# Queries projected by feature instead of by token in a fused gMLP and sliding-window attention trunk

## The chip, the core and the metric

The kernel runs on one core of a Trainium2 chip. A core has a matrix engine (TensorE, PE in the profile), a vector engine (VectorE, DVE), a scalar engine (ScalarE, ACT), GpSimd (POOL), and SyncE (SP), which here only issues transfers. Each engine works through its own queue in order, and semaphores tie the queues together. The metric is the device time of one execution in microseconds (us); the time of a kernel is the median of its runs.

## The reference

The input `x` has 2048 tokens of 1024 features in float32. Layer A is a gated MLP with a spatial mix over chunks of 128 tokens. Layer B is attention over a window of 128 tokens, with 16 query heads of 64 features, 2 key/value heads, rotary positions and one sink per head. What the change touches is the making of the queries in layer B:

```
z = rms_norm(h, b_norm_g) @ w_in          # (2048, 1024) @ (1024, 2048)
q, g = split(z, 2)
q = rotary((q + b_q) as 16 heads of 64, pos)
scores = q . k * 64**-0.5                 # each block of 128 queries against 256 keys
```

Rotary turns each head's features in two halves of 32: the first half becomes `x1*cos - x2*sin`, the second `x2*cos + x1*sin`.

## The kernel before

Activations lie with features on the partitions and tokens along the row, in float32. To keep accuracy with the faster matrix format, each operand is split in a high and a low part, and a product is three matmuls: high by high, high by low, low by high (`mm3`, lines 122 to 124).

Layer A takes the first part of the execution, up to about 1437 us. It also multiplies the weights of layer B by the norm's gain, splits them, and writes them back to memory (`pre_jobs` and `prescale`, lines 491 to 516; the multiply is line 504 on POOL). Layer B then runs four blocks of 512 tokens (loop at line 1140). In each block the list `PIECES` (line 53) gives the order of the projections: two pieces for keys and values (`k`), eight for queries (`q`, two for each of four quads of heads) and eight for the gate (`g`).

A clock `now` counts half pieces: `half()` (line 145) advances it by one and runs what is due. The scores of quad `q` and token tile `t` start at the half that `ATT` (line 54) gives, 11, 12, 14, 15 for the first quad, then 18, 20, 20, 22, then 23, 26, 28, 28, then 29, 31, 33, 35. `S_T` and `T_PV` halves later follow the transposes of the probabilities (line 1002) and the product with the values (line 1024). This is the order in which the program is written; the Tile scheduler decides, when the program is built, the fixed order in which each engine gets its instructions.

A `k` or `q` piece is token by feature: in `natural` (line 875) the activations of 128 tokens are the stationary operand and 256 columns of weights move, 24 matmuls for a token tile and 48 for a piece. A `q` piece holds four heads of two token tiles. DVE adds the bias (line 928) and rotates along the row (`rope`, lines 868 to 872); ACT and DVE split the result (lines 935 and 936). Three halves later (`Q_T`) TensorE transposes it, eight transposes a piece (line 943), and ACT copies it out (line 945), so that the features come to lie on the partitions, as the scores need them (lines 971 and 972).

A `g` piece is feature by token: `proj` (line 298) holds 128 by 128 weights stationary and moves 512 tokens, 24 matmuls for a piece, and ACT copies the bank out (line 951).

Weights come through `weights()`: it keeps three tiles ahead (`LOOKAHEAD`) in four buffers, and POOL issues the transfer (line 190). A `q` piece before takes two weight tiles for both of a quad's pieces. At the end of a block, `outproj_b` (line 1043) multiplies the gated attention by the output weights, which are split on ACT and DVE (lines 118 and 119). DVE also prepares the next block's normed activations there (`hn_steps`, line 323).

All temporary tiles of 128 by 512 come from one pool of 39 slots (`GEN_B`).

Of the kernel before, what the change touches and what calls it, by code (L numbers as in the profile page):

```python
# [12 lines left out]
F32 = mybir.dt.float32  # L13
# [5 lines left out]
P = 128  # L19
S = 2048  # L20
D = 1024
# [33 lines left out]
S_T = 4  # L55
T_PV = 3
K_T = 5
Q_T = 3
HN0 = 35


@with_exitstack
def trunk(ctx: ExitStack, tc: tile.TileContext, xT, wv, wug, wao, wkv, wqg, wbo, wsT, bs, gains, lngb,
          bq, bkv, sinks, rot, masks, out):
    nc = tc.nc
    V, A, G, PE = nc.vector, nc.scalar, nc.gpsimd, nc.tensor

# [265 lines left out]
    with ExitStack() as actx:  # L333
# [155 lines left out]


        pre_jobs = [(wkv[i], wkvD[i], kv_g[:, 4 * i:4 * i + 4], 4) for i in range(2)]
        pre_jobs += [(wqg[i], wqgD[i], b_g[:, 4 * (i % 2):4 * (i % 2) + 4], 4) for i in range(8)]
        pre_jobs += [(wqg[i], wqgD[i], b_g, 8) for i in range(8, 16)]

        def prescale(i):
            src, dst, g, nk = pre_jobs[i // 2]
# [350 lines left out]
    wraw[0] = ctx.enter_context(tc.tile_pool(name="raw", bufs=W_RAW_BUFS))  # L847
    msk = bc.tile([P, 3, P], F32, name="msk")
    nc.sync.dma_start(msk, masks)
    bq_sb = bc.tile([P, D], F32, name="bq_sb")  # L850
    nc.sync.dma_start(bq_sb, bq.partition_broadcast(P))
    bkv_sb = bc.tile([P, 256], F32, name="bkv_sb")
    nc.sync.dma_start(bkv_sb, bkv.partition_broadcast(P))
    sink_sb = bc.tile([P, 16], F32, name="sink_sb")
# [63 lines left out]

        after(K_T, turn)

    def q_piece(b, q, tp, w2, hh, hl, qT, tab):
        if not w2:
            w2.extend([weights(), weights()])
        ps = bank()
        for t2 in range(2):
            natural(ps, t2, 2 * tp + t2, w2, hh, hl)
        qs = slot()
        V.tensor_tensor(qs.rearrange("p (t n) -> p t n", t=2), ps.rearrange("p (t n) -> p t n", t=2),
                        bq_sb[:, None, q * 256:(q + 1) * 256].broadcast_to([P, 2, 256]), ALU.add)
        qr = rope(qs.rearrange("p (t h d) -> p t h d", t=2, h=4), 4, 2 * tp, 2, tab)  # L930
        qr = qr.rearrange("p (t h d) -> p t h d", t=2, h=4)
        sts = []
        for t2 in range(2):
            st = slot(F32R).rearrange("p (h s d) -> p h s d", h=4, s=2)
            A.copy(st[:, :, 0, :], qr[:, t2])
            V.tensor_tensor(st[:, :, 1, :], qr[:, t2], st[:, :, 0, :].bitcast(F32), ALU.subtract)
            sts.append(st)

        def turn():
            for t2 in range(2):  # L940
                pst = bank().bitcast(F32R)
                for h in range(4):
                    PE.transpose(pst[:, h * P:(h + 1) * P], sts[t2][:, h].rearrange("p s d -> p (s d)"), ident_r)  # L943
                t = slot(F32R)
                A.copy(t, pst.bitcast(F32))
                qT[4 * q + 2 * tp + t2] = t

        after(Q_T, turn)

    def g_piece(i, sg, hh, hl):  # L950
        A.copy(sg[:, i, :], proj(hh, hl))
# [1 line left out]
    def scores(b, q, t, qT):  # L953


        c = b * TT + t
        cur, prv = c % RING, (c - 1) % RING
        ic = int(cur != 0)
        band = slice(0, RING, RING - 1) if cur == 0 else slice(prv, cur + 1)
        kv = q // 2  # L960
        mx = sm.tile([P, 4], F32, name="mx")
        den = sm.tile([P, 4], F32, name="den")
        pn = slot()
        pss = []
        for par in range(2):
            ps = bank()
            for i in range(2):
                o = ps[:, i * 256:(i + 1) * 256]
                h = 2 * i + par
                lq = qT[4 * q + t][:, h * P:(h + 1) * P]  # L970
                PE.matmul(o, lq, kst[:, kv, 0, band, :], start=True, stop=False)  # L971
                PE.matmul(o, lq, kst[:, kv, 1, band, :], start=False, stop=True)  # L972
            s4 = ps.rearrange("p (i a k) -> p i a k", i=2, a=2)
            own, sel = s4[:, :, ic, :], s4[:, :, 1 - ic, :]
            if c == 0:
                V.copy_predicated(sel, msk[:, 1, None, :].broadcast_to([P, 2, P]).bitcast(I32),
                                  msk[:, 2, None, :].broadcast_to([P, 2, P]))
            V.copy_predicated(sel, msk[:, 0, None, :].broadcast_to([P, 2, P]).bitcast(I32), own)
            V.tensor_reduce(mx[:, 2 * par:2 * par + 2], sel, mybir.AxisListType.X, ALU.max)
            pss.append(sel)  # L980
        sk = sink_sb[:, 4 * q:4 * q + 4]
        m = sm.tile([P, 4], F32, name="m")
        V.scalar_tensor_tensor(m, mx, SC, sk, ALU.mult, ALU.max)
        nm = sm.tile([P, 4], F32, name="nm")
        V.tensor_scalar(nm, m, -1.0, None, ALU.mult)
        es = sm.tile([P, 4], F32, name="es")
        V.tensor_tensor(es, sk, m, ALU.subtract)
        for i in range(4):
            A.activation(pn[:, i * P:(i + 1) * P], pss[i // 2][:, i % 2, :], AF.Exp, bias=nm[:, i:i + 1], scale=SC,
                         accum_out=den[:, i:i + 1])  # L990
# [149 lines left out]
    for b in range(NB):  # L1140
        tab = slot().rearrange("p (a t d) -> p a t d", a=2, t=TT)
        nc.sync.dma_start(tab, rot[b])
        hh, hl = hn0
        qT, yh, yl = {}, {}, {}
        os_, sgs = {}, {}
        kvw, qw = [], {q: [] for q in range(NQ)}
        h0 = now[0]

        halves_done = [0] * NQ
# [30 lines left out]
        for p in PIECES:  # L1180
            kind, i, j = p[0], int(p[1]), int(p[2])
            if kind == "k":
                kv_piece(b, j, kvw, hh, hl, tab)
            elif kind == "q":
                q_piece(b, i, j, qw[i], hh, hl, qT, tab)
            else:
                if j == 0:
                    sgs[i] = qp.tile([P, 2, TB], F32, name="sg")
                g_piece(j, sgs[i], hh, hl)
                if j == 1:  # L1190
                    finish_quad(i)
# [5 lines left out]
def _layout(i):  # L1197
# [13 lines left out]
    wo = w_out.reshape(2, 2, 4, P, 2, 4, P)  # L1211
    a["wao"] = c(wo.transpose(0, 5, 4, 1, 3, 2, 6)).reshape(8, 4, P, 512)
    a["wkv"] = c(w_kv.reshape(2, 4, P, 256).transpose(0, 2, 1, 3)).reshape(2, P, 1024)
    wq = c(bw_in[:, :D].reshape(2, 4, P, 4, 256).transpose(3, 0, 2, 1, 4)).reshape(8, P, 1024)
    wg = c(bw_in[:, D:].reshape(KD, P, KD, P).transpose(2, 1, 0, 3)).reshape(8, P, 1024)
    a["wqg"] = np.concatenate([wq, wg])
    wo1 = c(bw_out[:, :512].reshape(4, 2, P, 512).transpose(0, 2, 1, 3)).reshape(4, P, 1024)
# [7 lines left out]
    a["bq"] = c(f("b_bq")[0])  # L1225
# [5 lines left out]
    cs = np.concatenate([cs, cs], axis=-1)  # L1231
    a["rot"] = c(cs.reshape(NB, TT, P, 2, HD).transpose(0, 2, 3, 1, 4))
    qi, kj = np.arange(P)[:, None], np.arange(P)[None, :]
    a["masks"] = c(np.stack([kj <= qi, kj > qi, np.zeros((P, P))], axis=1).astype(np.float32))
# [2 lines left out]


_INS = ["xT", "wv", "wug", "wao", "wkv", "wqg", "wbo", "wsT", "bs", "gains", "lngb", "bq", "bkv", "sinks",
        "rot", "masks"]  # L1240


def build(arrays):
# [17 lines left out]
```

## Time and profile before

| What | Value |
|---|---|
| Median of 3 runs | 2227.95 us (2225.21 to 2232.17) |
| Profiled execution, its own time | 2234.51 us |
| Its span, first to last instruction | 2232.8 us |
| Mean granted TensorE clock | 0.98 |
| Busy: PE, weight loads, DVE, ACT, POOL | 2141.1, 1813.6, 1669.6, 1088.6, 1092.5 us |
| Layer B | from about 1437 us to the end |

In a row of the groups stand the line, the engine, the operation, output and inputs by the program's names, the shapes with the count, then busy time and mean time of one, then the idle time just before them with its releasers. In a row of the windows stand the stretch, its length, then the busy time with the count of PE, weight loads, DVE, ACT and POOL, the granted clock, the share of the DMA engines and GB/s. In a row of the timeline stand the start, the duration, the engine, the line and the operation. A duration of a matmul holds its whole way through the array; matmuls follow each other faster than that, so their pace is read from their starts.

### The profile page before, as it was taken

To read this page: it belongs to the slowest core of one execution; us is meant where nothing else is said; L and a number is where in the kernel's file an instruction comes from. 1 tells how busy PE (TensorE), PEld (TensorE's weight loads), DVE (VectorE), ACT (ScalarE), POOL (GpSimd) and SP (SyncE) were. 2 spreads that over 40 slices of the span, in tenths; PEclk is the share of its full clock that TensorE was granted. 3 is DMA by queue.
4 is the path that set the end of the run, shared out by engine and by line. 5 is a ranking of instruction groups with operands and counts; after the bars stand their busy time and mean duration, and the time that the engine had idled before them with its cause. 6 is when DMAs were issued, how large, how long until landed. Compare 5 with 4: busy or idle time off the path is not lost.

```text
span 2232.8 us, 33563 instructions
## 1 busy us (share of the span) xinstructions
PE 2141.1 (96%) x11196; PEld 1813.6 (81%) x11196; DVE 1669.6 (75%) x2670; ACT 1088.6 (49%) x2431; POOL 1092.5 (49%) x1201
## 2 busy tenths in 40 slices
PE   7879999999899989999999899999999999999997
PEld 6658888888688767788888788898899889889986
DVE  7946787788986865756656977578867967986785
ACT  6224654445444534444444533246635734663573
POOL 4892355767444555644544545334514622551460
PEclk9989999999999999999999999999999999999999
DMA  8987555667786789634444786633363355337322
GB/s 283 342 298 238 180 185 188 208 196 244 256 303 226 273 312 314 222 113 135 149 133 130 263 309 214 214 123 114 123 245 115 115 187 180 114 124 243 116 95 95
DMA packets 208941, 441.96 MB, mean 198 GB/s; under 512 B 22656, under 2 KB 61824, under 8 KB 199552
## 3 DMA queue, kind: packets, MB, share of 16 engines
q1 hardware_dynamic: 163488, 255.76, 35.6%
q0 software_dynamic: 40672, 175.66, 21.5%
q10 hardware_dynamic: 4608, 8.39, 1.0%
q8 instruction: 89, 1.46, 0.3%
q14 instruction: 84, 0.69, 0.1%
HBM read 322.81 MB, written 116.92 MB: 197 GB/s over the span
## 4 chain that ended last, share of the span: by engine, by line
PE 72%; DVE 10%; DMA 7%; issue 5%; POOL 4%; ACT 2%; SPq 1%; POOLq 0%; DVEq 0%; ACTq 0%
PE ps L130 13%; PE ps L129 13%; PE ps L128 13%; PE ps L122 8%; PE ps L123 8%; PE ps L124 8%; PE ps L635 2%; PE ps L1024 2%; DVE wa L119 1%; PE ps L971 1%; PE ps L1002 1%; PE ps L972 1%; PE ps L943 1%; DMA s<-Y 1%; POOL qa L479 1%
## 5 line engine op out<-in xcount | busy, mean ns | idle before, releaser
L119 DVE TENSOR_TENSOR wa<-w_raw,wa 128x512 fp32r<-128x512 f32 x456 | 478.7, 1059 | 148.0 <-ACT wa L118 147.0
L130 PE MATMUL ps<-xh,wa 128*128 128x512 f32 x1344 | 529.4, 394 | 14.7 <-DVE wa L119 14.7
L128 PE MATMUL ps<-xh,wa 128*128 128x512 f32 x1344 | 531.2, 395 | 0.6 <-DVE s L656 0.3
L129 PE MATMUL ps<-xl,wa 128*128 128x512 f32 x1344 | 528.2, 393 | 0.0
L118 ACT CAST wa<-w_raw 128x512 fp32r<-128x512 f32 x456 | 280.6, 619 | 433.0 <-PE ps L130 314.9
L130 PEld LDWEIGHTS ps<-xh,wa 128*128 128x128 f32 x1344 | 253.3, 188 | 74.8 <-DVE wa L119 18.4
L128 PEld LDWEIGHTS ps<-xh,wa 128*128 128x128 f32 x1344 | 253.6, 189 | 56.6 <-DVE s L656 0.8
L129 PEld LDWEIGHTS ps<-xl,wa 128*128 128x128 f32 x1344 | 253.6, 189 | 55.7
L1010 POOL TENSOR_SCALAR_AFFINE_SELECT s<-s 128x512 fp32r<-128x512 f32 x256 | 185.0, 750 | 101.5 <-ACT s L1004 70.2
L223 POOL TENSOR_TENSOR w_raw<-w_raw 128x512 f32<-128x512 f32 x48 | 78.6, 1639 | 224.5 <-DMA w_raw<-in_wug 121.7
L122 PE MATMUL ps<-w,hn 128*128 128x256 f32 x640 | 184.5, 288 | 0.0
L123 PE MATMUL ps<-w,hn 128*128 128x256 f32 x640 | 182.6, 285 | 0.0
L124 PE MATMUL ps<-w,hn 128*128 128x256 f32 x640 | 182.5, 285 | 0.0
L119 DVE TENSOR_TENSOR xl<-s,xh 128x512 fp32r<-128x512 f32 x168 | 137.7, 856 | 13.7 <-ACT xh L118 13.6
L190 POOL DMA_DIRECT2D w<-wb x72 | 40.5, 563 | 208.8 <-PE ps L124 177.7
L631 ACT ACTIVATE vp<-vp,nb,rs 128x128 f32<-128x128 f32 x256 | 106.6, 485 | 46.0 <-DMA vp<-v 39.1
L123 PE MATMUL ps<-wa,xh 128*128 128x512 f32 x256 | 107.1, 418 | 21.2 <-DVE wa L119 20.9
L996 POOL TENSOR_TENSOR s<-s,rd 128x512 f32<-128x512 f32 x64 | 69.5, 1088 | 114.8 <-ACT s L1004 46.6
L123 PEld LDWEIGHTS ps<-w,hn 128*128 128x128 f32 x640 | 124.4, 194 | 0.5
L122 PEld LDWEIGHTS ps<-w,hn 128*128 128x128 f32 x640 | 124.2, 194 | 0.5
L124 PEld LDWEIGHTS ps<-w,hn 128*128 128x128 f32 x640 | 124.2, 194 | 0.0
L225 POOL TENSOR_TENSOR w_raw<-w_raw 128x512 f32<-128x512 f32 x48 | 65.1, 1362 | 104.7 <-DVE wa L119 102.4
(192 smaller groups left out, 5007.6 us busy)
## 6 DMA issues: line engine op xcount, KB each, us to landing
w<-wb POOLq DMA_DIRECT2D x72, 1024.0 KB, 5.5
w_raw<-in_wug SPq DMA_DIRECT2D x160, 256.0 KB, 3.2
w_raw<-in_wv SPq DMA_DIRECT2D x88, 256.0 KB, 5.4
s<-in_xT SPq DMA_DIRECT2D x80, 256.0 KB, 4.7
w_raw<-in_wao SPq DMA_DIRECT2D x80, 256.0 KB, 4.2
wb<-s POOLq DMA_DIRECT2D x72, 256.0 KB, 5.1
vp<-v SPq DMA_DIRECT2D x32, 512.0 KB, 4.4
Y_s<-s POOLq DMA_DIRECT2D x64, 256.0 KB, 3.9
```

Of the source, the lines that this page charges most:

```text
L118: A.copy(hi, src)
L119: (lo_eng or V).tensor_tensor(lo, src, hi.bitcast(F32), ALU.subtract)
L122: PE.matmul(ps, ah, bh, start=first, stop=False)
L123: PE.matmul(ps, ah, bl, start=False, stop=False)
L124: PE.matmul(ps, al, bh, start=False, stop=last)
L128: PE.matmul(ps, ah, bh, start=first, stop=False, skip_group_check=True)
L129: PE.matmul(ps, ah, bl, start=False, stop=False, skip_group_check=True)
L130: PE.matmul(ps, al, bh, start=False, stop=True, skip_group_check=True)
L223: G.tensor_tensor(u["22"], u["21"], u["22"], ALU.add)
L631: A.activation(v[:, c, :], v[:, c, :], AF.Identity, bias=nb[:, c:c + 1], scale=rs[:, c:c + 1])
L996: G.tensor_tensor(p4, p4, rd[:, :, None].broadcast_to([P, 4, P]), ALU.mult)
L1010: G.affine_select(out=y.rearrange("p (h q) -> p h q", h=4), in_=x.rearrange("p (h q) -> p h q", h=4), pattern=[[0, 4], [sign, P]], base=ba ...
```

## The change

A `q` piece now makes 128 features (two heads) for all 512 tokens of a block, with `proj`, as the `g` pieces do. The features come out on the partitions, so the transposes and their copies are gone. The rotation needs the other half of each head, which now lies 32 partitions away: ACT copies the bank in four pieces of 32 partitions to a tile with the halves exchanged. DVE then does bias and multiply in one instruction for the bank and one for the exchanged copy, adds the two, and the split runs per head, with the low part written to the other 64 partitions. The rotation's table is transposed on the host (`rotT`) with the sign in it, and comes as two more tiles of 128 by 512 in every block. The bias comes as 16 values for each partition instead of a row of 1024 copied to all partitions. A quad's four tiles `qT` each hold one head for all 512 tokens, where each before held four heads of one token tile. The query weights' gain is laid out as the gate's.

```
-        pre_jobs += [(wqg[i], wqgD[i], b_g[:, 4 * (i % 2):4 * (i % 2) + 4], 4) for i in range(8)]
-        pre_jobs += [(wqg[i], wqgD[i], b_g, 8) for i in range(8, 16)]
+        pre_jobs += [(wqg[i], wqgD[i], b_g, 8) for i in range(16)]
...
-    bq_sb = bc.tile([P, D], F32, name="bq_sb")
-    nc.sync.dma_start(bq_sb, bq.partition_broadcast(P))
+    bq_sb = bc.tile([P, 2, KD], F32, name="bq_sb")
+    nc.sync.dma_start(bq_sb, bq)
...
-    def q_piece(b, q, tp, w2, hh, hl, qT, tab):
...
+    def q_piece(j, hh, hl, qT, tabT):
+        ps = proj(hh, hl)
+        a, r = slot(), slot()
+        for to in range(0, P, 32):
+            fr = to ^ 32
+            A.copy(r[to:to + 32], ps[fr:fr + 32])
+        V.scalar_tensor_tensor(a, ps, bq_sb[:, 0, j:j + 1], tabT[0], ALU.add, ALU.mult)
+        V.scalar_tensor_tensor(r, r, bq_sb[:, 1, j:j + 1], tabT[1], ALU.add, ALU.mult)
+        V.tensor_tensor(a, a, r, ALU.add)
+        for h in range(2):
+            t = slot(F32R)
+            s, o = slice(h * HD, (h + 1) * HD), slice((1 - h) * HD, (2 - h) * HD)
+            A.copy(t[s], a[s])
+            V.tensor_tensor(t[o], a[s], t[s].bitcast(F32), ALU.subtract)
+            qT[2 * j + h] = t
...
-                lq = qT[4 * q + t][:, h * P:(h + 1) * P]
+                lq = qT[4 * q + h][:, t * P:(t + 1) * P]
...
+        tabT = [slot(), slot()]
+        for i in range(2):
+            nc.sync.dma_start(tabT[i], rotT[b, i])
...
-                q_piece(b, i, j, qw[i], hh, hl, qT, tab)
+                q_piece(2 * i + j, hh, hl, qT, tabT)
```

The constant `Q_T` goes with the transposes. `PIECES`, `ATT` and the other times stay as they are.

More of the change, by code (lines that the diff above doesn't have):

```diff
@@ L63, in trunk @@
 def trunk(ctx: ExitStack, tc: tile.TileContext, xT, wv, wug, wao, wkv, wqg, wbo, wsT, bs, gains, lngb,
-          bq, bkv, sinks, rot, masks, out):
+          bq, bkv, sinks, rot, rotT, masks, out):
     nc = tc.nc
@@ L919, in kv_piece @@
         after(K_T, turn)
-    def q_piece(b, q, tp, w2, hh, hl, qT, tab):
[L922 to L948, printed above, removed]
+    def q_piece(j, hh, hl, qT, tabT):
[13 more added lines that the diff above has]
+            qT[2 * j + h] = t
     def g_piece(i, sg, hh, hl):
@@ L1145, in trunk @@
         os_, sgs = {}, {}
-        kvw, qw = [], {q: [] for q in range(NQ)}
+        kvw = []
         h0 = now[0]
@@ L1213, in _layout @@
     a["wkv"] = c(w_kv.reshape(2, 4, P, 256).transpose(0, 2, 1, 3)).reshape(2, P, 1024)
-    wq = c(bw_in[:, :D].reshape(2, 4, P, 4, 256).transpose(3, 0, 2, 1, 4)).reshape(8, P, 1024)
+    wq = c(bw_in[:, :D].reshape(KD, P, KD, P).transpose(2, 1, 0, 3)).reshape(8, P, 1024)
     wg = c(bw_in[:, D:].reshape(KD, P, KD, P).transpose(2, 1, 0, 3)).reshape(8, P, 1024)
@@ L1224, in _layout @@
     a["lngb"] = c(np.stack([f("a_ln_g")[0], f("a_ln_b")[0]]).reshape(2, NJ, P).transpose(2, 0, 1))
-    a["bq"] = c(f("b_bq")[0])
+    bqt = f("b_bq")[0].reshape(KD, P).T
+    a["bq"] = c(np.stack([bqt, bqt.reshape(2, 2, 32, KD)[:, ::-1].reshape(P, KD)], axis=1))
     a["bkv"] = c(f("b_kv"))
@@ L1231, in _layout @@
     cs = np.concatenate([cs, cs], axis=-1)
+    ct = cs.reshape(NB, TB, 2, HD).transpose(0, 2, 3, 1).copy()
+    ct[:, 1, :HD // 2] *= -1
+    a["rotT"] = c(np.concatenate([ct, ct], axis=2))
     a["rot"] = c(cs.reshape(NB, TT, P, 2, HD).transpose(0, 2, 3, 1, 4))
@@ L1239 @@
 _INS = ["xT", "wv", "wug", "wao", "wkv", "wqg", "wbo", "wsT", "bs", "gains", "lngb", "bq", "bkv", "sinks",
-        "rot", "masks"]
+        "rot", "rotT", "masks"]
 def build(arrays):
```

1 line of the change is left out of this document (removed).

## The prediction

> **What bounds the kernel now.** I read the page first, then the busy time by stretch for one block of layer B, then TensorE's timeline, then who waited for whom, and the chain of waits last.
>
> ```profile
> PE 2141.1 (96%) x11196; PEld 1813.6 (81%) x11196; DVE 1669.6 (75%) x2670; ACT 1088.6 (49%) x2431; POOL 1092.5 (49%) x1201
> ...
> L119 DVE TENSOR_TENSOR wa<-w_raw,wa 128x512 fp32r<-128x512 f32 x456 | 478.7, 1059 | 148.0 <-ACT wa L118 147.0
> ```
>
> ```profile
> 1652.00:1750.00 98.00, 97.09 (x720) 91.02 (x720) 78.01 (x197) 53.55 (x170) 39.67 (x58) 1.00 0.43 151
> 1750.00:1808.00 58.00, 56.63 (x308) 47.59 (x307) 53.32 (x97) 42.00 (x105) 31.01 (x34) 1.00 0.36 119
> ...
> 2140.00:2192.00 52.00, 51.91 (x305) 45.06 (x304) 38.94 (x81) 37.09 (x98) 28.04 (x35) 1.00 0.31 94
> ```
>
> ```profile
> 1700.00:1720.00 20.00, 19.26 (x142) 17.76 (x140) 18.81 (x50) 10.07 (x39) 9.50 (x14) 1.00 0.44 159
> ...
> 1740.00:1760.00 20.00, 19.86 (x120) 17.10 (x119) 18.87 (x49) 16.87 (x48) 8.56 (x13) 1.00 0.20 67
> ```
>
> The change touches layer B alone. There TensorE has hardly any gap: 97.09 of 98 us where most queries are made, at full clock. What is taken from TensorE should come off the time, as long as nothing else is as full. DVE is the candidate. It is at 80% in the first row, but at 94% in both of the 20 us rows and at 92% in the second row, where a block ends.
>
> ```profile
> PE ps L915 <- ACT s L902: 4.7, 1, 4.7
> PE ps L122 <- ACT s L118: 3.6, 3, 1.3
> PE ps L943 <- ACT s L989: 3.2, 8, 0.6
> ...
> PE ps L943 <- DVE s L936: 1.9, 1, 1.9
> ```
>
> ```profile
> 1772.62 0.96 PE ps L1024 x8
> ...
> 1804.01 1.24 DVE o L1037
> ...
> 1806.00 0.96 PE ps L122 x3
> ```
>
> TensorE's waits in layer B are short: 4.7 us at its start, 5.1 us (3.2 + 1.9) ahead of the query transposes, 3.6 us at the ends of three blocks. The chain at one such end leaves TensorE at 1772.6 and runs almost wholly through DVE, to return at 1806.0. TensorE loses little there only because it has the first three quarters of the output projection meanwhile. Were TensorE 8 us earlier and DVE not, it would wait those 8 us.
>
> **The change, part by part: TensorE.** The paces come from starts in the timeline of the second block.
>
> ```profile
> 1657.07 0.40 PE L122 MATMUL ps<-hn,w 128*128 128x512 f32 x1
> ...
> 1660.91 0.85 PE L943 MATMUL ps<-ident_r,s 128*128 128x128 f32 x8
> 1661.60 0.46 PE L122 MATMUL ps<-hn,w 128*128 128x512 f32 x1
> 1661.90 0.39 PE L123 MATMUL ps<-hn,w 128*128 128x512 f32 x1
> ...
> 1664.42 0.28 PE L122 MATMUL ps<-w,hn 128*128 128x256 f32 x1
> ...
> 1667.29 0.28 PE L971 MATMUL ps<-kst,s 128*128 128x256 f32 x1
> ```
>
> ```profile
> 1472.62 0.64 PE ps L943 x8
> ```
>
> ```profile
> L943 PE MATMUL ps<-ident_r,s 128*128 128x128 f32 x256 | 28.3, 247 | 5.2 <-ACT s L989 3.2 <-DVE s L936 1.9
> ```
>
> Between 1661.90 and 1664.42 lie 11 matmuls of 512 columns: 229.1 ns each. Between 1664.42 and 1667.29 lie 24 of 256 columns: 119.6 ns each. A query piece took 48 x 119.6 = 5.74 us and will take 24 x 229.1 = 5.50 us. Over 32 pieces that is 7.8 us less.
>
> The Trainium skill, "TensorE: Matmul & The Clock Gate", section Back-to-back issue gap, gives a warm matmul N/2.4 + 2.5 ns, so 109.2 and 215.8 ns: the estimate by it is 2.6 ns for each pair joined, 2.0 us over the 768 pairs, in place of 7.8. The trace disagrees, as both widths run 10 to 13 ns above that, so each matmul saved is worth more here.
>
> The 256 transposes are 32 groups of eight. A group took 0.64 us in one place and 0.69 (1660.91 to 1661.60) in another, and the first matmul behind holds the array 0.30 where 0.23 is usual. I take 0.72 a group: 23.0 us. Together TensorE loses 30.8 us of work, 0.96 us a piece, 7.7 us a block. The 5.1 us of waits ahead of the transposes lose their place; the scores need the same data only a little later, so I credit 2 us of it (bounds 0 and 5.1).
>
> **DVE and ACT.** The groups that price the old and new steps, where the shapes are kept apart:
>
> ```profile
> L119 DVE TENSOR_TENSOR s<-o,s 128x512 fp32r<-128x512 f32 x32 | 25.7, 826 | 4.5 <-ACT s L118 4.3
> L868 DVE TENSOR_TENSOR s<-s 128x512 f32<-128x512 f32 x32 | 24.7, 772 | 0.9
> L869 DVE TENSOR_TENSOR s<-s 128x512 f32<-128x512 f32 x32 | 23.5, 734 | 0.0
> L928 DVE TENSOR_TENSOR s<-ps,bq_sb 128x512 f32<-128x512 f32 x32 | 21.9, 683 | 3.6 <-PE ps L124 3.3
> L871 DVE TENSOR_TENSOR s<-s 128x256 f32<-128x256 f32 x32 | 19.2, 601 | 0.4
> L872 DVE TENSOR_TENSOR s<-s 128x256 f32<-128x256 f32 x32 | 18.8, 587 | 0.0
> L936 DVE TENSOR_TENSOR s<-s 128x256 fp32r<-128x256 f32 x64 | 25.7, 442 | 6.5 <-ACT s L935 6.5
> L637 DVE SCALAR_TENSOR_TENSOR s<-ps,lngb_sb,wc 128x512 f32<-128x512 f32 x64 | 46.1, 743 | 19.7 <-PE ps L635 19.7
> L1075 DVE SCALAR_TENSOR_TENSOR s<-s,g_sb 128x512 f32<-128x512 f32 x24 | 16.2, 747 | 0.1
> L935 ACT CAST s<-s 128x256 fp32r<-128x256 f32 x64 | 22.8, 405 | 74.5 <-DVE s L872 74.5
> L945 ACT CAST s<-ps 128x512 fp32r<-128x512 f32 x64 | 34.3, 594 | 0.0
> L118 ACT CAST s<-o 128x512 fp32r<-128x512 f32 x32 | 18.5, 617 | 13.0 <-DVE o L1037 12.7
> ```
>
> DVE before, a piece: 683 + 772 + 734 + 601 + 587 + 2 x 442 = 4261 ns. After: 743 for the bank, 747 for the exchanged copy, 772 for the sum, 2 x 826 for the low parts = 3914 ns. Half the partitions don't make an instruction shorter by themselves; I price the 64-partition ones by their 512 columns. DVE gains 0.35 us a piece, 2.8 a block. Had I priced the two low parts by L936 it would gain 1.1 a piece, and by the page's weight split in layer A, the slowest subtraction of this shape (1059), it would lose 0.1.
>
> ACT before: 2 x 405 + 2 x 594 = 1998 ns. After: four copies of 32 partitions and two casts of 64. No row has 32 partitions by 512. The nearest are L945 by columns (594) and L935 (405) as a floor; I take 594, as time goes with the columns. So 4 x 594 + 2 x 617 = 3610 ns, 1.6 us more a piece, 12.9 a block (floor 0.9 a piece). In the 98 us row ACT goes from 53.55 to 66.4 of some 90 us. That lies beside TensorE's work, with room, so I cost it at nothing by itself. Without that cover it would be 4 x 12.9 = 52 us.
>
> **From the last matmul to a usable query**: 4 x 0.594 + 0.743 + 0.747 + 0.772 + 0.617 + 2 x 0.826 = 6.9 us, if no queue is in the way and DVE's first reading of the bank comes behind the four copies. The first quad's last matmul precedes 1657.07 and its first scores start at 1667.29, so 10.2 us lie between. The late quads have a queue:
>
> ```profile
> 1730.96 0.28 PE L971 MATMUL ps<-kst,s 128*128 128x256 f32 x1
> ...
> 1748.58 0.39 PE L971 MATMUL ps<-kst,s 128*128 128x256 f32 x1
> ```
>
> ```profile
> 1740.39 0.67 DVE L928 TENSOR_TENSOR s<-ps,bq_sb 128x512 f32<-128x512 f32 x1
> ```
>
> The last query piece ends at 1730.96, DVE takes it up at 1740.39, and the quad's scores start at 1748.58: 17.6 us, of which the queue has 9.4 and the new chain 6.9. That leaves 1.3 us.
>
> The Trainium skill, "PSUM — Partial Sum Buffer", section PSUM bank collisions raise a hardware error, has it that two engines may not touch one bank and quadrant at once, reads included. That speaks against this form, since ACT's copies and DVE's first instruction read one bank: by it the chain is 6.9 us, and without it 6.2. No run here shows what two readers at once would do.
>
> **What is given back.** From 1700 to the block's end DVE has some 7% free. Four of the eight pieces fall in there, with 3.9 us of TensorE's saving; DVE's own work shrinks by only 4 x 0.35 = 1.4 us there, and ACT's grows. I let blocks one to three give back 3 us each (bounds 0 and 7.7) and the last 1 us, since DVE is at 75% in its end (38.94 of 52, no next block to prepare): 10 us.
>
> **Transfers and queues.**
>
> ```profile
> s<-in_rot SPq DMA_DIRECT2D x4, 256.0 KB, 9.1
> bq_sb<-in_bq SPq DMA_DIRECT2D x1, 512.0 KB, 9.4
> ```
>
> SP issues two more loads in each block, 2 MB in all. The like of them lands in 9.1 us, and a block has its key pieces before it needs them; if they came late, DVE would wait up to 9 us a block. The 512 KB of bias ahead of the key bias at layer B's start go, behind which TensorE waits its 4.7 us (L915): I credit 1 us (bounds 0 and 3). The gain's multiply in layer A keeps its tile and its count: nothing. Weight transfers stay 72, taken one a piece instead of two, so POOL waits for a free buffer less; I credit nothing.
>
> **The sum**, against the profiled execution's own 2234.5: -23.0 - 7.8 - 2 - 1 + 10 = -23.8, so 2210.7. That execution lies 6.6 above the median of the three runs, 2227.95, on whose scale I predict 2204.
>
> **The rivals.**
>
> *All of it arrives.* If DVE's small gain and its idle time suffice, nothing is given back and the waits ahead of the transposes go too: 30.8 + 5.1 + 1 = 37 less, 2191. The 80% row of DVE speaks for it, the 94% rows against.
>
> *DVE and ACT pace the block.* The block's end stays where DVE's chain (1772.6 to 1806.0) puts it, and that chain follows DVE from 1700 on. Then each of the first three blocks gives its 7.7 us back, against 3 in the forecast; only the last keeps it, and 7 to 10 us remain: 2219, or 2227 if ACT's longer queue holds up DVE by 2 us a block more. For it speaks that DVE already waits for casts (L936, 6.5 us); against it, that its last stretch holds no query work.
>
> *Slower: the scores wait for late queries.* TensorE takes its instructions in a set order, so scores whose query isn't ready block all matmuls behind. There are 16 quads. With the queue of 9.4 us seen in the last quad and 1.3 us left, 4 us of extra delay on ACT for a quad would do. It decides from 34/16 = 2.1 us a quad, 34 being the forecast's gain with nothing given back; at 3 us it costs 48 and the time is 2228 - 34 + 48 = 2242. Against it: the first quads have 3 us and more of slack, and the scheduler sets scores later where its plan sees the query late.
>
> **How the numbers follow.** Forecast 0.52, all of it 0.17, paced 0.20, slower 0.11. Its own range is 2196 to 2213. The range that holds 8 in 10 goes from 2191 to 2229: it takes in the full saving and the paced block, and leaves out most of the slower case. A difference under 0.3% (about 7 us, the spread of the runs before) can't be told from no change. Faster by more than that needs under 2221: the forecast, all of it, and half of the paced case, 0.79. Same: 0.11. Slower: 0.10.
>
> **What would show it.** The changed profile should have no transposes of queries, 768 more matmuls of 512 columns and 1536 fewer of 256 in layer B, at 229 ns. The copies by 32 partitions should be near 594 ns, ACT up by some 50 us, DVE down by some 11. Layer B's four blocks should each be shorter by 5 us (the last by 7), and TensorE's waits for ACT's cast at the blocks' ends should grow from 1.2 us to about 4. I am wrong if scores (L971's successor) head the list of TensorE's waits, if the new table comes late, or if the 39 slots run out, since a quad's four queries now live until its last scores.

## The result and the profile after

The changed kernel takes 2277.65 us (median of 4 runs, 2276.09 to 2280.49) against 2227.34 us of the kernel before beside it: a ratio of 1.022 [1.0205, 1.0235]. It is 50 us slower, where 24 us faster was forecast. The profiled execution spans 2278.8 us, before 2232.8.

First the page's busy times, then the stretch from the start of layer B to the end, first of the kernel after and then of the kernel before.

```profile
PE 2136.7 (94%) x10172; PEld 1767.7 (78%) x10172; DVE 1643.4 (72%) x2606; ACT 1152.6 (51%) x2495; POOL 1083.3 (48%) x1201
```

```profile
1437.00:2300.00 863.00, 767.52 (x4046) 648.00 (x4044) 581.64 (x1287) 488.63 (x1250) 295.59 (x398) 0.95 0.39 133
```

```profile
1437.00:2300.00 863.00, 769.02 (x5076) 694.69 (x5074) 599.49 (x1353) 423.95 (x1186) 300.91 (x398) 0.99 0.38 132
```

Counted from 1437 us, layer B lasted 842 us after (2278.8 - 1437) and 796 before; its first key projections start at 1422 us after and at 1424 before. So the whole loss is there. TensorE was busy for nearly the same time, 768 and 769 us, although it had some 31 us less to do: its granted clock was 0.95 in place of 0.99. ACT has 65 us more and DVE 18 less.

The new operations' groups, shapes kept apart (kernel after, layer B):

```profile
L926 ACT COPY s<-ps 32x512 f32<-32x512 f32 x128 | 73.9, 577 | 1.9
L934 DVE TENSOR_TENSOR s<-s 64x512 fp32r<-64x512 f32 x64 | 43.9, 686 | 17.1 <-ACT s L933 15.4
L933 ACT CAST s<-s 64x512 fp32r<-64x512 f32 x64 | 39.4, 616 | 40.8 <-DVE s L929 40.0
L927 DVE SCALAR_TENSOR_TENSOR s<-ps,bq_sb,s 128x512 f32<-128x512 f32 x32 | 24.0, 749 | 34.3 <-ACT s L926 34.2
L928 DVE SCALAR_TENSOR_TENSOR s<-s,bq_sb 128x512 f32<-128x512 f32 x32 | 23.8, 743 | 0.0
L929 DVE TENSOR_TENSOR s<-s 128x512 f32<-128x512 f32 x32 | 21.9, 685 | 0.6
```

The durations are what the forecast took, or less: a piece costs ACT 4 x 577 + 2 x 616 = 3540 ns (3610 forecast), and DVE 749 + 743 + 685 + 2 x 686 = 3549 ns (3914). Behind the second bar stands what it did not take: DVE stands idle for 34.2 us ahead of its first reading of the bank, until ACT's four copies are done, and for 15.4 us until the casts are. The Trainium skill, "PSUM — Partial Sum Buffer", section PSUM bank collisions raise a hardware error, says that two engines must not read one bank and quadrant at once. The trace agrees in that L927 reads nothing that the copies write, and yet ends its idle time at their end. (A run below, e6, shows what becomes of this wait when both read another memory.)

Whom TensorE waited for (kernel after, from 1430 us on; total, times, longest):

```profile
PE ps L1011 <- POOL s L997: 17.7, 8, 3.7
PE ps L958 <- ACT s L976: 13.6, 4, 3.5
PE ps L958 <- DVE s L934: 6.0, 8, 2.2
PE ps L121 <- ACT s L117: 5.8, 3, 2.3
PE ps L913 <- ACT s L900: 4.7, 2, 3.7
PE ps L1011 <- issue: 3.5, 4, 0.9
PE ps L121 <- DVE s L992: 3.3, 4, 0.9
```

All rows of this view add to 66 us, those of before to 18. The late queries themselves (L934) are only 6.0 of them. The two largest lie further on in the softmax: the values (L1011) wait for POOL's selection of the transposed probabilities (L997), and scores (L958) wait for exponentials (L976), by the tile's name for a bank that these still read.

One such wait, followed through the timeline of the second block, with rows left out between the ones shown:

```profile
1673.68 5.39 DVE L1062 SCALAR_TENSOR_TENSOR s<-s,g_sb 128x512 f32<-128x512 f32 x8
1679.53 0.39 PE L121 MATMUL ps<-hn,w 128*128 128x512 f32 x1
1681.29 1.28 ACT L976 ACT_TABLE_LOAD   x1 [7.33 <-DVE es L974]
1685.00 0.29 PE L958 MATMUL ps<-kst,s 128*128 128x256 f32 x1
1685.70 2.35 ACT L926 COPY s<-ps 32x512 f32<-32x512 f32 x4
1691.30 1.26 ACT L933 CAST s<-s 64x512 fp32r<-64x512 f32 x2 [2.05 <-DVE s L929]
1692.58 0.37 ACT L976 ACTIVATE s<-ps,nm 128x128 f32<-128x128 f32 x1
1694.11 2.34 ACT L926 COPY s<-ps 32x512 f32<-32x512 f32 x4
1696.49 0.75 DVE L927 SCALAR_TENSOR_TENSOR s<-ps,bq_sb,s 128x512 f32<-128x512 f32 x1 [1.98 <-ACT s L926]
1698.61 1.06 ACT L1022 ACTIVATE sg<-sg 128x1024 f32<-128x1024 f32 x1
1700.20 1.40 DVE L934 TENSOR_TENSOR s<-s 64x512 fp32r<-64x512 f32 x2 [1.58 <-ACT s L933]
1703.51 0.61 ACT L991 ACTIVATE s<-ps 128x512 fp32r<-128x512 f32 x1
1705.19 4.74 POOL L997 TENSOR_SCALAR_AFFINE_SELECT s<-s 128x512 fp32r<-128x512 f32 x8
1705.88 0.58 PE L1011 MATMUL ps<-s,vst 128*128 128x256 f32 x1 [3.71 <-POOL s L997]
```

TensorE keeps its timetable: 24 matmuls from 1679.53 to 1685.00, 228 ns each, end the query piece q11. ACT stands still for 7.33 us, because the exponentials at the head of its queue need DVE, which is busy with eight multiplies of the previous block's norm (L1062). In the kernel before, the same eight multiplies were over by 1666.74, before the block's first scores at 1667.29:

```profile
1661.35 5.39 DVE L1075 SCALAR_TENSOR_TENSOR s<-s,g_sb 128x512 f32<-128x512 f32 x8
```

The first copies at 1685.70, of the piece before q11, are ready but stand behind the exponentials. Those of q11 start at 1694.11, 9 us after its last matmul, and the query is done at 1701.6: 16.6 us, where the chain without queues would take 2.34 + 0.75 + 0.74 + 0.69 + 0.62 + 1.40 = 6.5. The copy of the transposed probabilities (L991) then comes behind all of it, at 1703.51, POOL's selection after that, and TensorE waits 3.71 us. Not all that stands ahead of that copy is new: the gate's copy and activation (L1022) and their table loads were there before the change.

What such a wait does to the clock (windows, then TensorE's timeline, kernel after):

```profile
1758.00:1764.00 6.00, 5.85 (x16) 4.67 (x17) 5.08 (x12) 3.62 (x8) 2.48 (x4) 0.55 0.01 3
```

```profile
1755.70 0.39 PE L958 MATMUL ps<-kst,s 128*128 128x256 f32 x1 [3.38 <-ACT s L976]
...
1758.75 0.63 PE L122 MATMUL ps<-hn,w 128*128 128x512 f32 x1
...
1763.01 0.60 PE L123 MATMUL ps<-hn,w 128*128 128x512 f32 x1
```

After an idle time of 3.38 us (and one of 0.70 us soon behind it), ten matmuls of 512 columns take 4.26 us (1758.75 to 1763.01): 426 ns each in place of 228. So the wait cost 3.4 us, and the slow matmuls behind it some 2.4 us more. The Trainium skill, "TensorE: Matmul & The Clock Gate", section The HAM clock gate, tells of a halved clock after about 3.4 us without work and gives 426.7 ns for this width. The trace agrees with the pace (426 ns), and nearly with the idle time (3.38 us).

The sum of the three: TensorE's work -31, its waits +48 (18 to 66), and the clock some +30, together +47 for a layer B that is 46 us longer. The term of the clock is an estimate: in windows of 10 us from 1437 on, the time times what the granted clock lacks of 1 adds up to 39 us after and 9 before.

### The profile page after: what moved, and what is told of

It reads as the page before. It is cut to its first block, busy times and chain, and to the rows that moved or that the text cites. A ratio compares the mean times of both kernels' runs of the same rounds, so it can differ in the third digit from the quotient of the medians.

```text
span 2278.8 us, 31453 instructions
## 1 busy us (share of the span) xinstructions
PE 2136.7 (94%) x10172; PEld 1767.7 (78%) x10172; DVE 1643.4 (72%) x2606; ACT 1152.6 (51%) x2495; POOL 1083.3 (48%) x1201
## 4 chain that ended last, share of the span: by engine, by line
PE 42%; DVE 8%; ACT 6%; issue 2%; DMA 1%; POOL 1%; SPq 0%; POOLq 0%; DVEq 0%; ACTq 0%
PE ps L129 7%; PE ps L128 7%; PE ps L127 7%; PE ps L121 6%; PE ps L122 6%; PE ps L123 6%; PE ps L1011 2%; ACT s L926 1%; ACT s L976 1%; PE ps L633 1%; PE ps L958 1%; POOL s L997 1%; ACT s L933 1%; DVE ps L965 1%; PE ps L959 1%
## 5 line engine op out<-in xcount | busy, mean ns | idle before, releaser
L118 DVE TENSOR_TENSOR wa<-w_raw,wa 128x512 fp32r<-128x512 f32 x456 | 472.5, 1046 | 150.5 <-ACT wa L117 149.2
L117 ACT CAST wa<-w_raw 128x512 fp32r<-128x512 f32 x456 | 280.4, 618 | 418.2 <-PE ps L129 312.4
L997 POOL TENSOR_SCALAR_AFFINE_SELECT s<-s 128x512 fp32r<-128x512 f32 x256 | 181.1, 736 | 109.5 <-ACT s L991 82.7
L121 PE MATMUL ps<-hn,w 128*128 128x512 f32 x512 | 211.2, 412 | 6.2 <-DVE s L992 3.3
L122 PE MATMUL ps<-hn,w 128*128 128x512 f32 x512 | 207.0, 404 | 0.0
L123 PE MATMUL ps<-hn,w 128*128 128x512 f32 x512 | 206.3, 403 | 0.0
L122 PE MATMUL ps<-wa,xh 128*128 128x512 f32 x256 | 106.0, 414 | 23.1 <-DVE wa L118 23.1
L121 PEld LDWEIGHTS ps<-hn,w 128*128 128x128 f32 x512 | 100.4, 196 | 26.3 <-DVE s L992 4.5
L123 PEld LDWEIGHTS ps<-hn,w 128*128 128x128 f32 x512 | 100.1, 195 | 21.3
L117 ACT CAST xh<-s 128x512 fp32r<-128x512 f32 x168 | 97.5, 617 | 36.9 <-DMA s<-X_s 10.2
L122 PEld LDWEIGHTS ps<-hn,w 128*128 128x128 f32 x512 | 100.5, 196 | 17.5
```

The costliest lines, as they stand in the source:

```text
L117: A.copy(hi, src)
L118: (lo_eng or V).tensor_tensor(lo, src, hi.bitcast(F32), ALU.subtract)
L121: PE.matmul(ps, ah, bh, start=first, stop=False)
L122: PE.matmul(ps, ah, bl, start=False, stop=False)
L123: PE.matmul(ps, al, bh, start=False, stop=last)
L997: G.affine_select(out=y.rearrange("p (h q) -> p h q", h=4), in_=x.rearrange("p (h q) -> p h q", h=4), pattern=[[0, 4], [sign, P]], base=ba ...
```

## The experiments

Each ratio is against the kernel before on the same chip (2227 to 2231 us). The first theory was A: ACT's copies stand in its queue ahead of the softmax and make it late. Its rivals were B, that the queries come too late by their longer chain, and P, that their bank is held too long. Four came with the later runs: T, that the softmax's work on the vector engines sets the pace between two turns; W, that TensorE's work adds to the path; O, that the order of the work in the queues costs; L, that ACT's added work is too much wherever it stands. A turn is what the attention has TensorE do at a set half: a token tile's scores, its transposes, or its values.

**The exchange alone (e2).** The changed kernel with the rotation reading the bank unexchanged:

```
-        for to in range(0, P, 32):
-            fr = to ^ 32
-            A.copy(r[to:to + 32], ps[fr:fr + 32])
-        V.scalar_tensor_tensor(r, r, ...)
+        V.scalar_tensor_tensor(r, ps, ...)
```

> The changed kernel without the exchange: DVE's second bias-and-multiply reads the bank straight, so the rotation pairs each feature with itself; the exchange is left out of the computation. ACT loses 2.3 us a piece, DVE's count stays as in the changed kernel. Theory A: 2193 to 2215, since the copies are the only thing that stood in the way. Theory B: the chain falls from 6.9 to 4.6 us, less than a third, and the time to 2225 to 2255.

2219.51 us, 0.9964 [0.9949, 0.9979]. The exchange costs 58 us (2277.65 - 2219.51): ACT's copies, DVE's idle time until they are done, and what follows from both. Neither theory has this time in its range. And without the exchange only 8 of TensorE's 31 us arrive. Of the waits this is what heads the list:

```profile
PE ps L1008 <- POOL s L994: 8.1, 12, 2.9
PE ps L121 <- ACT s L117: 6.0, 3, 2.5
```

The values (L1008 here) wait 8.1 us for POOL's selection, where in the kernel before (L1024) it was half a microsecond:

```profile
PE ps L1024 <- POOL s L1010: 0.5, 2, 0.3
```

**The copies added to the kernel before (e3).** Four copies of 32 partitions a query piece, out of its bank, which nothing reads:

```
+        r = slot()
+        for to in range(0, P, 32):
+            fr = to ^ 32
+            A.copy(r[to:to + 32], ps[fr:fr + 32])
```

> The kernel before with four copies of 32 partitions by 512 from the query's bank on ACT in each of the 32 query pieces; nothing reads the copies. ACT gains 2.3 us a piece, the same as the change adds, while queries keep their old chain. Theory A: slower by 20 to 50 us, 2250 to 2278, with TensorE waiting for the softmax's steps. Theory B: within 8 us of the kernel before, 2220 to 2236.

2258.78 us, 1.0135 [1.0112, 1.0157]: 30 us, as theory A expected, for 74 us of work on an engine that was busy half the time.

```profile
PE ps L122 <- ACT s L933: 15.0, 8, 3.5
PE ps L122 <- ACT s L118: 6.7, 3, 4.2
```

Here the copies (L933) hold their bank so long that the projection itself (L122) waits for it. Work of the kind that the forecast set to nothing costs 30 us without anything else of the change. It isn't the same path, though: in the changed kernel no row has the projection wait for the copies.

**TensorE's saving alone (e8).** The kernel before without its 256 query transposes; ACT copies the untransposed split at the same place instead:

```
-                pst = bank().bitcast(F32R)
-                for h in range(4):
-                    PE.transpose(pst[:, h * P:(h + 1) * P], sts[t2][:, h]..., ident_r)
...
-                A.copy(t, pst.bitcast(F32))
+                A.copy(t, sts[t2]....bitcast(F32))
```

> The kernel before without the 256 transposes of the queries: ACT's copy at the same place reads the untransposed split instead of the transposed bank, so the scores get wrong queries; DVE and ACT do the same number of instructions of the same width. TensorE loses 23 us of work. If TensorE paces layer B: 2200 to 2209. If the vector side paces it: 2220 to 2230.

2252.62 us, 1.0106 [1.0083, 1.0128]. Taking 23 us of work from the fullest engine made the kernel 23 us slower, which no theory had expected.

```profile
PE ps L968 <- ACT s L942: 16.8, 10, 3.6
PE ps L968 <- ACT s L986: 10.0, 3, 3.3
PE ps L1021 <- POOL s L1007: 5.9, 11, 1.2
```

The scores come too early for ACT's copies (L942) and for the exponentials (L986).

**The same with 256 transposes of a constant (e9)**, which nothing reads, so that TensorE has its work back:

```
+                pst = bank().bitcast(F32R)
+                for h in range(4):
+                    PE.transpose(pst[:, h * P:(h + 1) * P], ident_r, ident_r)
```

> The kernel before without its query transposes (2252.6 us in an earlier run), with 256 transposes of the constant identity put back in their place; nothing reads them, so TensorE has its 23 us of work back and waits for no query there. The rest is as in that run. Theory T (the softmax work between the vector engines sets the pace of layer B; TensorE work between its turns only fills the time, and taking it out makes TensorE arrive early, wait, and lose clock): the filler costs nothing or brings time back, 2225 to 2245 us, and the waits for ACT L942 and L986 (26.8 us) fall to under 12. Theory W (TensorE's work adds to the path, the loss came from somewhere else): 2252.6 + 23 = about 2275 us.

2244.53 us, 1.0064 [1.0041, 1.0086]. 23 us of work was given back and the time fell by 8, as theory T expected. Theory W, which asks for 2275, is out: this work was filling, not pace. Of the 23 us that e8 lost, then, 8 go with the missing work. The longest wait for the copies fell from 3.6 to 0.7 us:

```profile
PE ps L1024 <- POOL s L1010: 5.7, 8, 1.2
...
PE ps L971 <- ACT s L945: 2.8, 5, 0.7
```

The other 16 us down to the kernel before aren't explained; what still differs is that ACT's copies read another tile (622 ns each against 594, under 2 us in all), and the orders that the scheduler then gives. These orders differ between e8 and e9, too, so the 8 us rest on one pair of kernels.

**Other ways to make the exchange (e1, e5, e6).** First by DVE, which reads the bank shifted in four instructions, with no copy on ACT:

```
-            A.copy(r[to:to + 32], ps[fr:fr + 32])
-        V.scalar_tensor_tensor(r, r, bq_sb[:, 1, j:j + 1], tabT[1], ...)
+            V.scalar_tensor_tensor(r[q], ps[fr:fr + 32], bq_sb[q, 1, j:j + 1], tabT[1][q], ...)
```

> The changed kernel with the four exchange copies taken off ACT: DVE reads the other half's 32 partitions of the bank itself, in four bias-and-multiply instructions instead of one. The result is the same. ACT loses 4 x 0.577 = 2.3 us a piece, DVE gains 3 to 4 instructions of about 0.7 us, 2.1 us a piece. Theory A (the copies stand in ACT's queue ahead of the softmax's exponentials and copies, and make these late): the time falls to 2200 to 2230, TensorE's waits in layer B from 67 us to under 35. Theory B (the queries are late because their chain is long, whoever runs it): 2260 to 2285, and the waits stay above 55 us.

2302.41 us, 1.0327 [1.0306, 1.0348].

```profile
PE ps L957 <- DVE s L933: 16.1, 17, 2.2
PE ps L957 <- DVE o L1018: 12.4, 4, 3.5
```

ACT has no copy there and the loss is larger than both theories allowed, so it isn't ACT's queue alone: DVE, with 72 us more to do in layer B, has no more room than ACT has. Then by four transfers on SP's queue, out of one copy of the bank (e5), and by four ACT copies out of such a copy (e6):

```
+        A.copy(c, ps)
...
-            A.copy(r[to:to + 32], ps[fr:fr + 32])
+            nc.sync.dma_start(r[to:to + 32], c[fr:fr + 32])    # or A.copy
```

> The changed kernel with the bank copied out once by ACT (128 by 512, about 0.59 us) and the exchange done by four transfers of 32 partitions from that copy, issued by SP. The result is the same. ACT loses 1.7 us a piece, DVE's count stays, the bank is free after one copy, the query's chain gets some 2 to 4 us longer. Theory A (work in ACT's queue) and theory P (the query's PSUM bank is held too long): 2205 to 2240. Theory B (the chain to the query is too long): 2277 or more.

> The changed kernel with the bank copied out once by ACT, and the four exchange copies then read that copy in SBUF instead of the bank; DVE reads the copy too. ACT gains 0.6 us a piece over the changed kernel, the chain gets 0.6 us longer, but the bank is free after 0.6 us instead of some 3. Theory P: 2235 to 2262. Theories A and B: 2285 to 2310.

2362.66 us, 1.0593 [1.0566, 1.062], and 2309.3 us, 1.0364 [1.0339, 1.039]. Freeing the bank early (theory P) doesn't help: the bank is free after one copy in both, and both are slower. Theory A is missed by the first as well, where ACT has 1.7 us a piece less to do and the time is 85 us longer. Both times lie where theory B put them.

In e6 DVE's first reading (L928 there) and ACT's copies both read the copy in SBUF:

```profile
L928 DVE SCALAR_TENSOR_TENSOR s<-s,bq_sb 128x512 f32<-128x512 f32 x32 | 27.8, 870 | 4.2 <-POOL s L998 2.4 <-ACT s L924 0.8
L929 DVE SCALAR_TENSOR_TENSOR s<-s,bq_sb 128x512 f32<-128x512 f32 x32 | 24.0, 750 | 55.9 <-ACT s L927 55.9
```

DVE no longer stands idle ahead of the first reading (4.2 us in place of 34.3), so in the changed kernel it was most likely the shared bank that held it there. But it then waits 55.9 us ahead of the second, which needs the exchanged copy. Sharing the bank decides where DVE waits, not that it waits.

**Are the queries late (e4, e7)?** Their pieces ahead of the gate's, with the attention's timetable as it was:

```
-PIECES = "k00 k01 q00 q01 g00 q10 q11 g01 q20 q21 g10 q30 q31 ..."
+PIECES = "k00 k01 q00 q01 q10 q11 g00 g01 q20 q21 q30 q31 g10 ..."
```

> The changed kernel with the order of pieces changed so that each quad's queries are made two to four half pieces (5 to 11 us) further ahead of their scores; the gate pieces move back. All instructions are the same. Theory B (late queries): TensorE's waits ahead of the scores (22 us) go, 2225 to 2250. Theory A (ACT's queue): the copies are as many, and the time stays at 2262 to 2285.

2272.39 us, 1.02 [1.0176, 1.0223], 5 us under the changed kernel: theory A's range, not B's. And with scores that read a constant tile, so that nothing waits for a query, while all its work is done:

```
-                lq = qT[4 * q + h][:, t * P:(t + 1) * P]
+                lq = qc[:, t * P:(t + 1) * P]
```

> The changed kernel with the scores reading one constant tile instead of the queries; the query pieces do all their work, nothing waits for it. The scores are left out of the computation in that sense. Theory B: 2195 to 2225, since no scores wait for a query. Theories A and P: 2260 to 2285, since ACT, DVE and the banks have the same work.

2290.18 us, 1.0271 [1.0245, 1.0297].

```profile
PE ps L1013 <- POOL s L999: 28.2, 12, 5.3
PE ps L960 <- ACT s L978: 14.7, 4, 3.8
PE ps L121 <- ACT s L117: 12.5, 3, 4.2
```

With no query to wait for, TensorE waits later, and longer: for the selection (L999), for exponentials (L978), and for the cast of the gated attention at the blocks' ends (L117). The time lies outside all three ranges; a direct wait of the scores for the query (theory B) isn't the cause.

**Time or order (e10 to e13)?** The same instructions in other orders. First the early queries with evenly spread scores, and the values half a piece later:

```
+ATT = [11, 12, 14, 15, 17, 18, 20, 21, 23, 24, 26, 27, 29, 30, 32, 33]
+T_PV = 4
```

> The changed kernel with another timetable: the queries' pieces ahead of the gate's, the sixteen scores spread evenly over halves 11 to 33, and the values 4 halves behind the transposes instead of 3. The same instructions in all. Theory T (the turns come too close for the vector side): the loss shrinks, 2235 to 2260 us, and the waits of the values for POOL's selection fall from 17.7 us to under 6. Theory L (the added ACT work itself is too much for the block, wherever the turns stand): 2268 to 2285 us.

2274.04 us, 1.0205 [1.0174, 1.0237].

```profile
PE ps L121 <- DVE s L992: 18.5, 8, 2.9
PE ps L989 <- DVE s L992: 14.9, 7, 3.1
```

The values' wait for the selection, 17.7 us, has left the head of the list, and 33 us for DVE's low part of the probabilities (L992) have come: the wait moved. The time is in theory L's range, not in T's. Then the scheduler's preference for the vector work of the softmax, for that of the query pieces, and for both:

```
+            with tc.high_priority(offset=300):
                 ... (the vector instructions of scores and turn_p, or of q_piece)
```

> The changed kernel, in which the scheduler is told to prefer the vector work of the softmax (from the selection of the scores to the selection of the transposed probabilities) over other work that is ready on ACT, DVE and POOL. The same instructions, another order on each engine. Theory O (what costs is the order in which ACT and DVE get the copies and the softmax; the copies stand ahead of the exponentials): 2235 to 2260 us, with the waits for ACT L976 and POOL L997 (together 31 us) under 15. Theory T, in which the amount of work between two turns is the limit: 2268 to 2285 us.

> The changed kernel, in which the scheduler is told to prefer the new work of a query piece (copies, rotation, casts) over other work that is ready on ACT and DVE. Theory B (late queries) expects 2245 to 2265 us. Theory O, with the copies ahead of the exponentials as the harm, expects the same or worse: 2275 to 2300 us. Theory T: within 10 us of the changed kernel's 2277.

> The changed kernel with both preferences at once: the query pieces' vector work and the softmax's ahead of everything else (key and value pieces, gates, weights, norms) that is ready on ACT, DVE and POOL. Theory O (the order in the queues of ACT and DVE is the loss): the two gains of 25.6 and 10 us add in part, 2230 to 2247 us. Theory T (what the softmax needs between two turns is the limit, and the query's gain came from taking its work out of the middle of a turn): both together are two claims on the same engines and cancel, 2250 to 2270 us.

2267.81 us (1.0174 [1.0154, 1.0195]), 2252.03 us (1.0106 [1.008, 1.0132]) and 2250.61 us (1.0102 [1.0082, 1.0123]). With the query pieces preferred half of the loss is gone; the softmax's preference adds nothing to that. The first time lies at the edge of T's range and the third in it, neither in O's. The second is outside the ranges of O and T, and in B's. But the scores' waits for queries hardly changed (4.8 us, 6.0 in the changed kernel), so B has the number and not the place. The waits of the second:

```profile
PE ps L1013 <- POOL s L999: 15.6, 10, 3.0
PE ps L122 <- ACT s L978: 12.3, 9, 2.4
```

No wait for the exponentials is above 2.4 us any more, where it was 3.5, and the mean clock is 0.981 against 0.969. Is the preference good for any such kernel? The kernel before with it (c12), and the change without its exchange with it (e16):

> The control: the kernel before with the same preference for the vector work of its query pieces. If the order's effect belongs to the changed kernel's longer chain on ACT (theory O as stated for the change), the kernel before stays within 5 us of its 2228 us. If any new order moves this kernel by tens of us, it moves by over 8 us either way.

> The changed kernel without the exchange of the rotation's halves (the rotation reads the bank as it stands, so the result is not the reference's), with the query pieces' vector work preferred. It ran at 2219.5 us without the preference, 8 us below the kernel before, where TensorE has 30.8 us less to do. Theory O: with a good order most of the saving arrives, 2195 to 2208 us. Theory T (the softmax's own time sets the pace): it stays at 2213 to 2222 us.

The kernel before goes to 2235.02 us, 1.0025 [1.0015, 1.0036], slightly worse and just outside theory O's 5 us. The change without its exchange stays at 2218.21 us, 0.9955 [0.9936, 0.9974], where it was 2219.51. So the preference gains nothing where the copies are missing, and theory O's 2195 to 2208 for the second is out: also with this order, 20 of the 31 us don't arrive, as theory T expected.

**What is left of the exchange (e14, e17, e18).** With the query order kept, values half a piece later (`T_PV = 4`, the last scores at 34):

> The changed kernel with the query pieces' vector work preferred (2252.0 us), and the values 4 halves behind the transposes instead of 3; the last turn starts at half 34 instead of 35, so that the output projection stands where it stood. Theory T: the values' wait for POOL's selection (15.6 us in that run) falls under 5 us, and 2225 to 2242 us. Theory O: the wait moves to another place, 2247 to 2257 us.

2279.3 us, 1.023 [1.0202, 1.0258], above both ranges: all of the gain is lost again, with new waits:

```profile
PE ps L122 <- DVE es L976: 12.9, 4, 3.2
PE ps L122 <- DVE s L929: 11.6, 4, 3.6
```

Last, ACT's two casts a piece taken to DVE, without and with the query order:

```
-            A.copy(t[s], a[s])
+            V.tensor_copy(t[s], a[s])
```

> The changed kernel with the two casts of a query piece (64 x 512, 616 ns on ACT) on DVE, so that after the four exchange copies a piece needs ACT no more: ACT's 3540 ns a piece become 2308 (before the change 1998), and two handovers between DVE and ACT go. DVE gets two operations more, of which no row has the length; the subtraction of that shape takes 686 ns, so at most 1.4 us a piece. Theory A (ACT's added time and the handovers): 2240 to 2260 us. Theory O (the place of the copies in the queue alone): 2268 to 2285 us.

> The same with the query pieces' vector work preferred, which stands at 2252.0 us with the casts on ACT. Theory A: 2220 to 2240 us, and TensorE's waits for ACT's exponentials (12.3 us in that run) fall to under 6. Theory O: 2246 to 2260 us, since the order is already the good one.

2267.28 us, 1.0172 [1.0151, 1.0194], and 2284.12 us, 1.025 [1.0212, 1.0289].

```profile
L933 DVE CAST s<-s 64x512 fp32r<-64x512 f32 x64 | 27.2, 425 | 2.1
```

A cast takes 425 ns there against 616 on ACT, and ACT has only 0.3 us a piece more than before the change. That gains 10 us at the scheduler's own order and loses 32 with the query pieces preferred. The same preference that gained 26 us with the casts on ACT costs 17 here. Theory A's figures are missed both times, so the loss isn't ACT's amount of work as such; those of theory O are missed too.

## Why the prediction was wrong

**"What is taken from TensorE should come off the time, as long as nothing else is as full."** This step failed. The row of 1652 to 1750 us, with 97.09 of 98 us, was read as "TensorE sets the pace". But transposes of a constant, put back, cost nothing (e8 to e9), and without the exchange 8 to 11 of 31 us arrive, at two different orders (e2, e16). The turns of the attention stand at fixed counts of projection work; what TensorE does between them is also the time in which DVE, ACT and POOL finish the softmax. Shortening it moves the next turn ahead of them, as the wait for POOL's selection says (0.5 us before, 8.1 in e2). In e2's trace TensorE's waits are 11 us longer than before, and the clock costs 2 us more; that covers 13 of the 23 us that stay away there (20 in e16), and the rest is open. The prediction saw this effect only for a block's end and allowed 10 us of give-back.

**"That lies beside TensorE's work, with room, so I cost it at nothing by itself."** This step failed hardest. The durations were right (577 measured for 594, 616 for 617), and the amount nearly: ACT has 65 us more where 52 were forecast, of which the new steps, 113 us against 57, make 56. The price was wrong: 74 us of such copies cost 30 us on the kernel before (e3), and the whole exchange costs 58 in the change (e2). The prediction's own figure without the cover, 52 us, lies near the 58 by luck: it is ACT's added time, while what was lost is TensorE's waits and its clock. A mean load of 58% (489 of 842 us) says nothing of an in-order queue: four copies that are ready stand behind exponentials that wait for DVE (7.33 us at 1681), and the next softmax stands behind the copies.

**DVE -0.35 us a piece.** The durations gave even more (4261 to 3549). Not counted was the idle time that the form makes: 34.2 us ahead of L927. The prediction had the copies ahead of DVE's first reading in its chain (6.9 us, measured 6.5 without queues), but as latency set against slack, not as time in which DVE's queue stands still. That is 1.1 us a piece beside the 0.7 saved; what this idle time costs by itself, no run shows.

**The slower rival** had the sign and not the place. It expected scores waiting for late queries, 2242 us. Only 6.0 us are of this kind, and a kernel without that wait is slower still (e7). Its 48 us of waits equal the measured growth by luck, as nearly all of these are other waits. And it left out the clock, which adds some 30 us.

**Smaller terms.** TensorE's pace at 512 columns held (228 ns against 229.1). The wait for ACT's cast at a block's end was forecast to grow from 1.2 to about 4 us; it grew to 1.9 (3.6 to 5.8 us in all). TensorE waited for no transfer of the new tables, and the wait at layer B's start, from which 1 us was credited, stayed at 4.7 us.

**What stays open.** Orders of the same instructions run from 2250.6 to 2279.3 us (seven kernels), so up to half of the 58 us of the exchange goes with the order. That it is the place of the copies in ACT's queue is likely and not shown: the preference moves DVE's work of a query piece, too. The rest, 34 us between e12 and e16, appears with the exchange in each order tried, and moving the casts didn't recover it. Whether a better order would, or the idle time of DVE ahead of its first reading (26.4 us in e12, too) must go first, isn't settled. Nor are the 16 us between e9 and the kernel before. No theory had all its times in range: A is missed by e1, e2, e5, e7, e17 and e18, B by e1 to e4 and e7, T by e10, e12 and e14, and O by every run made to test it. No version with the exchange in it beat the kernel before.

## What to carry to other kernels

A TensorE at 97% doesn't prove that TensorE sets the pace where its work stands at fixed counts between steps of a chain on other engines: add unread work to it, and if that is free, expect less than its length from removing work (8 to 11 of 31 us here). Work that a "half idle" in-order engine gets is to be priced by what stands behind it in that queue and by which engine must wait for it. Its full length belongs in the range, and isn't a sure upper bound: the forecast of 2204 us with its 52 us on top is 2256, and 2278 were measured. Where a change adds instructions to such an engine, try the order (a preference for the new work) before judging it; here that was worth 26 of 50 us. It isn't a rule: on two kernels without the copies it gained nothing, and with the casts on DVE it cost 17 us.

## What the runs showed of the hardware

- A copy of 32 partitions by 512 out of a bank takes ACT 577 ns, against 594 for 128 partitions: columns set the time. On DVE a subtraction of 64 partitions by 512 takes 686 ns, and a cast of that shape 425, against 616 on ACT.
- One idle time of 3.38 us on TensorE was followed by matmuls at 426 ns in place of 228 for some 5 us. Over layer B the clock fell from 0.99 to 0.95, by the estimate above some 30 us beside 48 us of added waits.
- Adding 23 us of unread TensorE work made a kernel 8 us faster (1.0106 [1.0083, 1.0128] to 1.0064 [1.0041, 1.0086]). The intervals just touch; the single runs don't (2249.8 to 2256.0 and 2241.3 to 2247.2 us).
